# Norm factors of q and k spread by TensorE, and bias rows of the sample group as long runs, in a one-core decoder layer

## The chip, the core and the metric

The kernel runs on one core of a Trainium2 chip. A core has five engines, each with its own in-order queue of instructions: TensorE (PE in the profile, with its weight loads as PEld), VectorE (DVE), ScalarE (ACT), GpSimd (POOL) and SyncE (SP), which here only issues transfers. Transfers are carried out by 16 DMA engines; those issued by SP form one queue, those issued by POOL another. The metric is the device time of one execution, in microseconds. Lower is better.

## The reference

One layer of a decoder that serves a prompt of 1024 tokens and 8 sample sequences of 8 tokens each, so 1088 tokens in all, with a model width of 1024:

```
a  = silu(c) @ w_ada + b_ada                  # 6 x 1024 shifts, scales, gates, per sequence
h  = rms_norm(x, g1) * (1 + scale1) + shift1
q, k, v, u = split(h @ w_in)                  # 512 columns each; q, k, v: 8 heads of 64
q  = rms_norm(q, q_g) * 64**-0.5              # by head
k  = rms_norm(k, k_g)
attn = three dilated window branches (window, step) = (128,1), (512,4), (2048,16),
       each softmax(q k + bias[bucket(distance)]), merged by their denominators;
       sample tokens read a cache of 2048 keys as well
pool = (trailing mean over 2/4/8/16 tokens - token) @ w_pool * pool_scale
x  = x + gate1 * (concat(attn, pool) @ w_out)
x  = x + gate2 * (relu(rms_norm(x) ... @ w_up)**2 @ w_down)
```

Outputs are the new x, the new k and v, the pooling input and the shifted caches. Everything is fp32. The norm by head is what the change touches: each head's 64 rows of q (or k) are multiplied, token by token, by one factor 1/sqrt(mean of squares + eps), and by a gain.

## The kernel before

Activations lie with features on the 128 partitions and the 1088 tokens along the free dimension. The tokens are cut into three chunks of 512, 288 and 288 columns (`CHUNKS`), since a PSUM bank holds 512 fp32 values per partition. There are eight such banks, all of one tag in the first phase (`ps`).

**Precision.** A product with a weight tile is made of three fp32r matmuls: the weight is split on the chip into a high part (ScalarE, L145) and the rest (VectorE, L146), the activations likewise, and high x high, low x high and high x low are summed (`gemm`, L236 to L245). Small products are plain fp32; each of those shows as two records in the profile.

**The order of work.** The source is traced in program order, and a scheduler (`schedule_with_timeline_sim=True`, L928) then chooses each engine's order by a model of the time, keeping the program order as priority and allotting the buffers. So neighbours in the source can be interleaved, and the engines' real queues are read from the trace.

**The start.** Eight tiles of x are loaded (L169), then `rel_bias`, and for a table of the bias by distance, in blocks of 1024 columns (`G0`, L176), a one-hot block `oh` and a block `lm` with the log of the number of branches (L180, L181). Distances number `GLEN` = 2312, so there are three blocks. Block n has its rows at partitions 32n. Small matmuls `pg` (L222) pick the bias, five in all, ScalarE copies them (L226), POOL adds them to `lm` (L300). The norm of x follows on TensorE (`n1`, L203). Once h is made, POOL writes the table to DRAM 16 times over (`gscr`, L305).

**The input projection** is the stage that the change is in. Its 16 column tiles of 128 are taken in the order k (tiles 4 to 7), q (0 to 3), u (12 to 15), v (8 to 11). `in_tile` (L309) loads a weight tile on SP's queue (`win4r` and so on, 512 KB), splits it, and multiplies into three PSUM banks `z`. It then takes two steps of the later part of the ada product (`ada_steps`, L117): each step loads a block of 512 KB on SP's queue (`wa`, L95) and multiplies it on TensorE (`pa`, L100). Eight steps share one PSUM bank `pa`; when the next eight begin, the old sum is copied and transposed (`pat`, L109). The weight blocks and the ada blocks share four buffers (`NRAW`).

`qk_group` (L321) runs four tiles, for k and then for q. For each tile VectorE copies z out of PSUM (L328) and ScalarE squares it (L329). After the fourth, twelve small matmuls against `sel` add the squares of each head (L337): the sums of tile r's two heads stand in rows 32r and 32r + 1. VectorE scales them (L338), and `rsqrt` (L136) with a Newton step (L131) gives the factors `rst`. POOL writes these to DRAM (`kscr` or `qscr`, four transfers of two rows, L342). SP reads each pair of rows back, repeated 64 times, as a full tile `rb` of 128 rows (L345). VectorE multiplies each tile with its gain and `rb` (L346). After the k group POOL writes k out (L352).

After the q group SP loads the bias rows of the sample tokens from `gscr`: `bs` for the cached keys and `bnew` for the new ones, by head pair (L360 to L372). A key of the cache is far if it is only in the branch of step 16: 96 groups of 8 keys, laid out group by group in the key tiles. A sample token's far bias is then 96 runs of 8 values (32 bytes each) in the table (L364 to L366).

u follows with the pooling sums on POOL (`pool_group`, L376), and its last pieces go out (`out_up` L380, `out_us` L412). Then v. After that come attention (phase 2), the output projection (phase 3) and the channel sub-layer (phase 4).

Of the kernel before, what the change touches and what calls it, by code (L numbers as in the profile page):

```python
# [38 lines left out]
GLEN = 2312  # L39
GREP = 16  # L40
# [8 lines left out]
def body(ctx: ExitStack, tc: tile.TileContext, i, o):  # L49
# [28 lines left out]
    cT, bT, g1T, g2T, qkg, ident, ones, sel, pscT, rcnt = (part(n) for n in CPK)  # L78
# [38 lines left out]
    def ada_steps():  # L117
        """the later 4096 columns, one block of rows a step"""
        done = None
        for r in (1, 2):  # L120
            for hf in range(2):
                pa = ps(f"pa{r}_{hf}")
                for k in range(KD):
                    ada_mm(pa, k, ada_load(r, hf, k, wpool, "raw", NRAW))
                    if k == 0 and done:
                        ada_end(*done)
                    yield
                done = (r, hf, pa)
        ada_end(*done)
# [6 lines left out]
    def rsqrt(r, v, t):  # L136
        """r = 1/sqrt(v)"""
# [34 lines left out]
    gscr = tc.dram_tile([H, GREP, GLEN], F32, name="gscr")  # L172
    rbias = const.tile([32, H], F32, tag="rbias", name="rbias")
    nc.sync.dma_start(rbias, i["rel_bias"])
    lm = nat_pool.tile([P, 1024], F32, tag="nat", name="lm")
    G0 = [(32 * n, c0, min(1024, GLEN - c0)) for n, c0 in enumerate(range(0, GLEN, 1024))]  # L176
# [19 lines left out]
    def rstd_of(acc, rstd, chunks, name):  # L196
        """rstd = 1/sqrt(mean + eps) on every partition, from the sums acc over feature blocks"""
# [105 lines left out]
    with tc.issue_after(ins.ins):  # L303
        for r0, c0, n in G0:
            G.dma_start(gscr[:, :, c0:c0 + n], lm[r0:r0 + H, :n].unsqueeze(1).to_broadcast([H, GREP, n]))  # L305

# [14 lines left out]
    def qk_group(base, gvec, name):  # L321
        """four tiles of two heads each: the projection, then the norm by head"""
        raws, sqs = [], []
        for r in range(4):
            outs = in_tile(base + r)
            t, sq = nat(f"{name}{r}"), nat(f"{name}sq{r}")
# [3 lines left out]
            raws.append(t)  # L330
            sqs.append(sq)
        rst = nat(f"{name}rst")
        vv, tv = nat(f"{name}vv"), nat(f"{name}tv")
        for ci, (c0, n) in enumerate(CHUNKS):
            pp = ps(f"{name}ss{ci}")
            for r in range(4):
                mm(pp[32 * r:32 * r + 32, :n], sel, sqs[r][:, c0:c0 + n], start=True, stop=True)  # L337
            V.tensor_scalar(vv[:, c0:c0 + n], pp[:, :n], 1.0 / E, EPS, ALU.mult, ALU.add)  # L338
        rsqrt(rst, vv, tv)
        scr = tc.dram_tile([H, T], F32, name=f"{name}scr")  # L340
        for r in range(4):
            G.dma_start(scr[2 * r:2 * r + 2, :], rst[32 * r:32 * r + 2, :])  # L342
        for r in range(4):
            rb = nat(f"{name}rb{r}")
            nc.sync.dma_start(rb, bass.AP(tensor=scr.tensor, offset=2 * r * T, ap=[[T, 2], [0, E], [1, T]]))  # L345
            V.scalar_tensor_tensor(raws[r], raws[r], gvec, rb, ALU.mult, ALU.mult)  # L346
        return raws

    kT = qk_group(4, gk, "k")

    for r in range(4):
        G.dma_start(o["kT"][r], kT[r])  # L352
    qT = qk_group(0, gq, "q")

# [5 lines left out]
    for hp in range(HP):  # L360
        r0 = 32 * hp
        g0 = 2 * hp * GREP * GLEN + TS - 1
        for a in range(2):
            nc.sync.dma_start(bs[r0 + a * TS:r0 + (a + 1) * TS, 0:NFAR].rearrange("p (n r) -> p n r", r=TS),  # L364
                              bass.AP(tensor=gscr.tensor, offset=g0 + a * GREP * GLEN,
                                      ap=[[GLEN - 1, TS], [16, 96], [1, TS]]))  # L366
        nc.sync.dma_start(bs[r0:r0 + 16, NFAR:NKEY],
                          bass.AP(tensor=gscr.tensor, offset=g0 + WB - NEAR,
                                  ap=[[GREP * GLEN, 2], [GLEN - 1, TS], [1, NEAR]]))
        nc.sync.dma_start(bnew[r0:r0 + 16, 7 * TS:8 * TS],  # L370
                          bass.AP(tensor=gscr.tensor, offset=g0 + WB,
                                  ap=[[GREP * GLEN, 2], [GLEN - 1, TS], [1, TS]]))  # L372
# [36 lines left out]
    for r in range(4):  # L409
        uT.append(in_copy(12 + r, f"u{r}"))  # L410
        pool_group(r)
    nc.sync.dma_start(o["us"], us[:, :, :, TS:])  # L412

    # v by token: a tile for each head pair, eight blocks of 128 tokens; the sample tokens of all heads
# [37 lines left out]
    def head_prep(h, pieces):  # L452
        """q and k of a head in two parts each: rows of the head, and the other rows"""
# [19 lines left out]
    # ================= phase 2: attention =================  # L473
# [13 lines left out]
    # sample queries by head pair: columns (head of the pair, token) over the rows of that head  # L487
# [15 lines left out]
    def softmax_tail(L, n, negm, name):  # L503
        """L holds minus the logits: L <- exp(logit - max); returns 1/sum"""
# [17 lines left out]
    def sample_S(b):  # L522
        """logits by 512 keys a step, then the softmax"""
# [21 lines left out]
    def sample_V(b):  # L545
        """the product with V by four tiles of 128 keys a step"""
# [403 lines left out]
```

## Time and profile before

| | |
|---|---|
| median of 3 runs | 1434.34 us (1432.61 to 1436.79) |
| span of the profiled execution | 1432.4 us |
| PE busy | 1316.1 us, 92% |
| PEld busy | 1130.7 us, 79% |
| DVE busy | 607.4 us, 42% |
| ACT busy | 402.6 us, 28% |
| POOL busy | 135.3 us, 9% |

The profile is of one further execution, whose span is the only time it has. Its views: the page (busy shares, and the span in 40 slices), who waited for whom, the chain of waits that ended last, the groups of instructions by line, the timeline of each engine, and the busy time, granted TensorE clock and DMA share in chosen stretches. In a timeline row the first number is the start, the second the length, both in us; `L337` is a line of the kernel; `z<-h1h,win2h` is output from inputs; `x3` counts records that were merged; `[11.07 <-ACT ...]` is the idle time before the row and what ended it. Rows of SPq are transfers being issued. A granted clock of 1.00 is full speed. DMA share is the mean busy share of the 16 engines.

### The profile page before, as it was taken

How to read it: one execution, taken by the hardware profiler on the slowest of the kernel's cores; microseconds unless marked ns; L12 is line 12 of the kernel's file. 1: busy time of each engine (PE TensorE's matmuls, PEld its weight loads, DVE VectorE, ACT ScalarE, POOL GpSimd, SP SyncE). 2: the span in 40 equal slices, each digit the busy share in tenths (PEclk: the TensorE clock that was granted, in tenths of full speed). 3: DMA queues.
4: the chain of work that ended last, by engine and by line, in shares of the span. 5: the costliest groups of instructions: out<-in, count | busy, mean ns of one | idle time of the engine just before them, and what ended most of it. 6: DMA issues, size and time to landing. Idle time of an engine off the chain costs nothing.

```text
span 1432.4 us, 21960 instructions
## 1 busy us (share of the span) xinstructions
PE 1316.1 (92%) x9230; PEld 1130.7 (79%) x9230; DVE 607.4 (42%) x1250; ACT 402.6 (28%) x705; POOL 135.3 (9%) x193
## 2 busy tenths in 40 slices
PE   3798469279899999999999999999999999999998
PEld 1586358168677776899999999999999999999998
DVE  5632121321576777465643343342433433424333
ACT  5322021011567676343420211202112112021120
POOL 2100000351232221000000000000000000000000
PEclk9899689599999999999999999999999999999999
DMA  9673432394986772556493181351631813511102
GB/s 296 236 94 90 143 129 80 106 137 139 329 270 237 254 259 64 208 168 216 157 331 113 45 278 44 131 193 44 222 102 45 278 45 132 191 47 43 45 17 109
DMA packets 65826, 217.27 MB, mean 152 GB/s; under 512 B 20824, under 2 KB 23040, under 8 KB 64704
## 3 DMA queue, kind: packets, MB, share of 16 engines
q1 hardware_dynamic: 62416, 143.31, 31.6%
q0 software_dynamic: 3312, 72.56, 15.7%
q8 instruction: 73, 1.20, 0.3%
q14 instruction: 25, 0.20, 0.0%
HBM read 203.31 MB, written 77.29 MB: 196 GB/s over the span
## 4 chain that ended last, share of the span: by engine, by line
PE 75%; ACT 2%; DMA 1%; DVE 1%; SPq 1%; issue 0%; POOL 0%; ACTq 0%; DVEq 0%; POOLq 0%
PE dn L243 9%; PE dn L241 9%; PE dn L245 9%; PE up L241 9%; PE up L243 9%; PE up L245 9%; PE po L617 2%; PE pt L612 2%; PE spo L566 1%; PE sl L533 1%; PE z L243 1%; PE ob L245 1%; PE ob L241 1%; PE ob L243 1%; PE z L245 1%; PE z L241 1%
## 5 line engine op out<-in xcount | busy, mean ns | idle before, releaser
L699 DVE SCALAR_TENSOR_TENSOR X<-dn,aT,X 128x512 f32<-128x512 f32 (+2 forms) x192 | 98.4, 567 | 204.6 <-PE dn L245 204.6
L731 POOL COPY mark<-fh 128x1 f32<-128x1 f32 x7 | 8.5, 1220 | 562.1 <-ACT fh L798 562.1
L617 PE MATMUL po<-PT,vtok 128*64 128x128 f32 x576 | 52.2, 287 | 4.7 <-ACT PT L615 3.9
L799 DVE TENSOR_TENSOR fl<-r,fh 128x1088 fp32r<-128x1088 f32 x32 | 41.3, 1292 | 35.5 <-ACT fh L798 35.5
L506 ACT ACTIVATE L<-L,m 128x128 f32<-128x128 f32 (+3 forms) x64 | 49.8, 778 | 22.5 <-DVE m L512 22.0
L617 PEld LDWEIGHTS po<-PT,vtok 128*64 128x64 f32 x576 | 33.7, 136 | 24.1 <-ACT PT L615 13.6
L100 PE MATMUL pa<-wa,cs 128*32 128x256 f32 x384 | 29.5, 407 | 22.6 <-DMA wa<-in_w_ada 22.5
L798 ACT CAST fh<-r 128x1088 fp32r<-128x1088 f32 x32 | 35.4, 1106 | 44.1 <-DVE r L795 44.1
L615 ACT COPY PT<-pt 128x512 f32<-128x512 f32 (+1 forms) x80 | 40.2, 541 | 15.6 <-PE pt L612 15.4
L243 PE MATMUL dn<-fh,wd_3l 128*128 128x288 f32 (+1 forms) x192 | 43.4, 328 | 0.0
L241 PE MATMUL dn<-fh,wd_3h 128*128 128x288 f32 (+1 forms) x192 | 43.4, 328 | 0.0
L245 PE MATMUL dn<-fl,wd_3h 128*128 128x288 f32 (+1 forms) x192 | 43.4, 328 | 0.0
L241 PE MATMUL dn<-fh,wd_1h 128*128 128x288 f32 (+1 forms) x192 | 42.5, 328 | 0.0
L243 PE MATMUL dn<-fh,wd_1l 128*128 128x288 f32 (+1 forms) x192 | 42.5, 328 | 0.0
L245 PE MATMUL dn<-fl,wd_1h 128*128 128x288 f32 (+1 forms) x192 | 42.3, 328 | 0.0
L243 PE MATMUL dn<-fh,wd_0l 128*128 128x288 f32 (+1 forms) x192 | 42.3, 328 | 0.0
L612 PE MATMUL pt<-cpk,L 128*128 128x128 f32 x288 | 41.6, 281 | 0.7 <-ACT L L506 0.4
L241 PE MATMUL dn<-fh,wd_0h 128*128 128x288 f32 (+1 forms) x192 | 42.2, 328 | 0.0
L243 PE MATMUL dn<-fh,wd_2l 128*128 128x288 f32 (+1 forms) x192 | 42.2, 328 | 0.0
L241 PE MATMUL dn<-fh,wd_2h 128*128 128x288 f32 (+1 forms) x192 | 42.2, 328 | 0.0
L245 PE MATMUL dn<-fl,wd_2h 128*128 128x288 f32 (+1 forms) x192 | 42.2, 328 | 0.0
L245 PE MATMUL dn<-fl,wd_0h 128*128 128x288 f32 (+1 forms) x192 | 42.1, 328 | 0.0
(947 smaller groups left out, 3482.9 us busy)
## 6 DMA issues: line engine op xcount, KB each, us to landing
out_kw<-in_cache_k POOLq DMA_DIRECT2D x8, 4080.0 KB, 15.6
out_vw<-in_cache_v POOLq DMA_DIRECT2D x8, 4080.0 KB, 28.6
wa<-in_w_ada SPq DMA_DIRECT2D x48, 512.0 KB
kc<-in_kc SPq DMA_DIRECT2D x40, 512.0 KB
vc<-in_vc SPq DMA_DIRECT2D x40, 512.0 KB
x<-in_xT SPq DMA_DIRECT2D x8, 544.0 KB
X<-in_xT SPq DMA_DIRECT2D x8, 544.0 KB
fs<-gscr SPq DMA_DIRECT2D x8, 512.0 KB
```

The source lines that it names most:

```text
L100: ins = mm(pa[32 * g:32 * g + 32, :256], cs[:, k, :], t[:, g // 2, (g % 2) * 256:(g % 2 + 1) * 256], start=(k == 0), stop=(k == KD - 1))
L241: mm(pt[:, :n], wh[:, kw], xh(k, c0, n), start=st, stop=False)
L243: mm(pt[:, :n], wl[:, kw], xh(k, c0, n), start=False, stop=False)
L245: mm(pt[:, :n], wh[:, kw], xl(k, c0, n), start=False, stop=sp)
L506: last["act"] = S.activation(L[:, :n], L[:, :n], AF.Exp, bias=negm, scale=-1.0, accum_out=sm)
L533: mm(pt[32 * hp:32 * hp + 32, c0:c0 + 256], qz[:, hp, b, :], kch[:, hp, :], start=True, stop=True)
L612: nc.tensor.transpose(pt[:, n * P:(n + 1) * P], Ls[ii][:, j * P:(j + 1) * P], ident)
L615: S.copy(PT[:, :w], pt[:, :w])
L617: mm(po[E * ii:E * ii + E, :P], v_blk(j, h * E, E), PT[:, n * P:(n + 1) * P], start=(j == 0), stop=(j == 2 * g + ii))
L699: V.scalar_tensor_tensor(X[:, m, c0:c0 + npr], pt[:, :npr], aT[:, base + m, 0:1], X[:, m, c0:c0 + npr], ALU.mult, ALU.add)
L798: S.copy(fh, r)
L799: V.tensor_sub(fl, r, f(fh))
```

## The change

1. `qk_group` becomes a class `QK` with three steps: `tile(r)`, `stats()` (up to the factors `rst`, as before) and `scale()`. `scale()` sends nothing through DRAM. For each chunk of tokens it takes four PSUM banks and lets TensorE multiply, for each tile r, a constant 32 x 128 matrix `selb` (one in row 0 for the first 64 columns, one in row 1 for the last 64) with rows 32r to 32r + 31 of `rst`. So each bank holds one tile's factors, spread to its 128 rows, and VectorE multiplies the tile with its gain and that bank, in place.
2. The scale stands one tile later in the source: k's after the first q tile, q's after the first u tile. k's four output transfers (POOL) follow k's scale.
3. The far keys of the cache are laid out by shift, all 96 groups of one of the eight positions after another (`rows`, on the host, for keys and values). A second table `fscr` of 15 x 96 distances is made beside the first, by the same matmuls, copies and additions, and written once to DRAM. A sample token's far bias is then one run of 768 values, so one transfer of 16 rows per head pair replaces two of 768 short runs.
4. The table grows from 2312 to 3752 columns: four blocks in place of three, eight matmuls `pg` in place of five.
5. The loads of `bs` and `bnew` move from SP's queue to POOL's: 12 transfers.
6. `selb` joins the packed constants. Comments are dropped.

```diff
+FLEN = 15 * 96
...
+    fscr = tc.dram_tile([H, FLEN], F32, name="fscr")
...
-    G0 = [(32 * n, c0, min(1024, GLEN - c0)) for n, c0 in enumerate(range(0, GLEN, 1024))]
+    G0 = [(32 * n, c0, min(1024, GLEN + FLEN - c0)) for n, c0 in enumerate(range(0, GLEN + FLEN, 1024))]
...
         for r0, c0, n in G0:
-            G.dma_start(gscr[:, :, c0:c0 + n], lm[r0:r0 + H, :n].unsqueeze(1).to_broadcast([H, GREP, n]))
+            ng = max(0, min(n, GLEN - c0))
+            if ng:
+                G.dma_start(gscr[:, :, c0:c0 + ng], lm[r0:r0 + H, :ng].unsqueeze(1).to_broadcast([H, GREP, ng]))
+            if ng < n:
+                f0 = c0 + ng - GLEN
+                G.dma_start(fscr[:, f0:f0 + n - ng], lm[r0:r0 + H, ng:n])
...
-        scr = tc.dram_tile([H, T], F32, name=f"{name}scr")
-        for r in range(4):
-            G.dma_start(scr[2 * r:2 * r + 2, :], rst[32 * r:32 * r + 2, :])
-        for r in range(4):
-            rb = nat(f"{name}rb{r}")
-            nc.sync.dma_start(rb, bass.AP(tensor=scr.tensor, offset=2 * r * T, ap=[[T, 2], [0, E], [1, T]]))
-            V.scalar_tensor_tensor(raws[r], raws[r], gvec, rb, ALU.mult, ALU.mult)
-        return raws
...
+        def scale(self):
+
+            for c0, n in CHUNKS:
+                c = slice(c0, c0 + n)
+                rbs = [ps(f"{self.name}rb{r}_{c0}") for r in range(4)]
+                for r in range(4):
+                    mm(rbs[r][:, :n], selb[32 * r:32 * r + 32, :], self.rst[32 * r:32 * r + 32, c], start=True, stop=True)
+                for r in range(4):
+                    V.scalar_tensor_tensor(self.raws[r][:, c], self.raws[r][:, c], self.gvec, rbs[r][:, :n], ALU.mult, ALU.mult)
+
+    kg, qg = QK(4, gk, "k"), QK(0, gq, "q")
+    kT, qT = kg.raws, qg.raws
+    for r in range(4):
+        kg.tile(r)
+    kg.stats()
+    qg.tile(0)
+    kg.scale()
     for r in range(4):
         G.dma_start(o["kT"][r], kT[r])
-    qT = qk_group(0, gq, "q")
...
+    for r in range(1, 4):
+        qg.tile(r)
+    qg.stats()
...
-        for a in range(2):
-            nc.sync.dma_start(bs[r0 + a * TS:r0 + (a + 1) * TS, 0:NFAR].rearrange("p (n r) -> p n r", r=TS),
-                              bass.AP(tensor=gscr.tensor, offset=g0 + a * GREP * GLEN,
-                                      ap=[[GLEN - 1, TS], [16, 96], [1, TS]]))
-        nc.sync.dma_start(bs[r0:r0 + 16, NFAR:NKEY],
+        G.dma_start(bs[r0:r0 + 16, 0:NFAR],
+                    bass.AP(tensor=fscr.tensor, offset=2 * hp * FLEN + 7 * 96,
+                            ap=[[FLEN, 2], [-96, TS], [1, NFAR]]))
+        G.dma_start(bs[r0:r0 + 16, NFAR:NKEY],
...
-        nc.sync.dma_start(bnew[r0:r0 + 16, 7 * TS:8 * TS],
+        G.dma_start(bnew[r0:r0 + 16, 7 * TS:8 * TS],
...
         uT.append(in_copy(12 + r, f"u{r}"))
+        if r == 0:
+            qg.scale()
         pool_group(r)
...
-    rows = np.concatenate([(16 * np.arange(96)[:, None] + np.arange(TS)[None]).ravel(), np.arange(WB - NEAR, WB)])
+    rows = np.concatenate([(16 * np.arange(96)[None] + np.arange(TS)[:, None]).ravel(), np.arange(WB - NEAR, WB)])
...
+    selb = np.zeros((P, P), np.float32)
+    selb[0::32, :E] = 1
+    selb[1::32, E:] = 1
```

More of the change, by code (lines that the diff above doesn't have):

```diff
@@ L76, in part @@
         return v
-    cT, bT, g1T, g2T, qkg, ident, ones, sel, pscT, rcnt = (part(n) for n in CPK)
+    cT, bT, g1T, g2T, qkg, ident, ones, sel, selb, pscT, rcnt = (part(n) for n in CPK)
     gq = const.tile([P, 1], F32, tag="gq", name="gq")
@@ L319, in in_tile, with __init__, tile @@
         return outs
-    def qk_group(base, gvec, name):
-        raws, sqs = [], []
-        for r in range(4):
-            outs = in_tile(base + r)
-            t, sq = nat(f"{name}{r}"), nat(f"{name}sq{r}")
+    class QK:
+        def __init__(self, base, gvec, name):
+            self.base, self.gvec, self.name = base, gvec, name
+            self.raws, self.sqs = [], []
+        def tile(self, r):
+            outs = in_tile(self.base + r)
+            t, sq = nat(f"{self.name}{r}"), nat(f"{self.name}sq{r}")
             for pt, (c0, n) in zip(outs, CHUNKS):
@@ L329, in qk_group @@
                 S.activation(sq[:, c0:c0 + n], pt[:, :n], AF.Square)
[L330 to L335, printed above, removed]
-            for r in range(4):
-                mm(pp[32 * r:32 * r + 32, :n], sel, sqs[r][:, c0:c0 + n], start=True, stop=True)
-            V.tensor_scalar(vv[:, c0:c0 + n], pp[:, :n], 1.0 / E, EPS, ALU.mult, ALU.add)
@@ L339, in qk_group @@
-        rsqrt(rst, vv, tv)
-        scr = tc.dram_tile([H, T], F32, name=f"{name}scr")
-        for r in range(4):
-            G.dma_start(scr[2 * r:2 * r + 2, :], rst[32 * r:32 * r + 2, :])
-        for r in range(4):
-            rb = nat(f"{name}rb{r}")
-            nc.sync.dma_start(rb, bass.AP(tensor=scr.tensor, offset=2 * r * T, ap=[[T, 2], [0, E], [1, T]]))
-            V.scalar_tensor_tensor(raws[r], raws[r], gvec, rb, ALU.mult, ALU.mult)
-        return raws
-    kT = qk_group(4, gk, "k")
+            self.raws.append(t)
@@ new lines, in tile, with stats @@
+            self.sqs.append(sq)
+        def stats(self):
+            name = self.name
+            rst = self.rst = nat(f"{name}rst")
+            vv, tv = nat(f"{name}vv"), nat(f"{name}tv")
+            for ci, (c0, n) in enumerate(CHUNKS):
+                pp = ps(f"{name}ss{ci}")
+                for r in range(4):
+                    mm(pp[32 * r:32 * r + 32, :n], sel, self.sqs[r][:, c0:c0 + n], start=True, stop=True)
+                V.tensor_scalar(vv[:, c0:c0 + n], pp[:, :n], 1.0 / E, EPS, ALU.mult, ALU.add)
+            rsqrt(rst, vv, tv)
@@ L351, in body @@
+    kT, qT = kg.raws, qg.raws
+    for r in range(4):
+        kg.tile(r)
+    kg.stats()
+    qg.tile(0)
+    kg.scale()
     for r in range(4):
         G.dma_start(o["kT"][r], kT[r])
-    qT = qk_group(0, gq, "q")
+    for r in range(1, 4):
+        qg.tile(r)
+    qg.stats()
     bs = side.tile([P, NKEY], F32, tag="bs", name="bs")
@@ L834 @@
 for _n, _s in (("cT", (KD, 9)), ("bT", (48,)), ("g1T", (KD,)), ("g2T", (KD,)), ("qkg", (2,)), ("ident", (P,)),
-               ("ones", (P,)), ("sel", (32,)), ("pscT", (4,)), ("rcnt", (4, CTX))):
+               ("ones", (P,)), ("sel", (32,)), ("selb", (P,)), ("pscT", (4,)), ("rcnt", (4, CTX))):
     CPK[_n] = (NCPK, _s)
@@ L851, in _distance_tables @@
 def _distance_tables():
-    dist = GOFF - np.arange(GLEN)
+    far = WB + 7 - np.arange(15)[:, None] - 16 * np.arange(96)[None]
+    dist = np.concatenate([GOFF - np.arange(GLEN), far.ravel()])
     d = np.maximum(dist, 1).astype(np.float32)
@@ L859, in _distance_tables @@
     logm = np.where(n > 0, np.log(np.maximum(n, 1)), BIG).astype(np.float32)
-    return onehot, np.ascontiguousarray(np.broadcast_to(logm, (H, GLEN)))
+    return onehot, np.ascontiguousarray(np.broadcast_to(logm, (H, GLEN + FLEN)))
 def _tiles(w, m):
@@ L894 @@
         "sel": sel,
+        "selb": selb,
         "pscT": col(pool_scale, 4),
```

## The prediction

> **What bounds the kernel now.** I read the page first: the engine totals, then the forty slices, each 35.8 us long.
>
> ```profile
> span 1432.4 us, 21960 instructions
> ...
> PE 1316.1 (92%) x9230; PEld 1130.7 (79%) x9230; DVE 607.4 (42%) x1250; ACT 402.6 (28%) x705; POOL 135.3 (9%) x193
> ...
> PE   3798469279899999999999999999999999999998
> ...
> PEclk9899689599999999999999999999999999999999
> ```
>
> TensorE is the bound, and from the tenth slice on it has hardly a hole. The holes are in the slices from 143 to 322 us (digits 4, 6, 9, 2, 7), where the input projection runs, and there the granted clock falls as well. So I asked who TensorE waited for up to 380 us (columns: total us, times, longest).
>
> ```profile
> PE z L241 <- ACT qsq L329: 25.3, 1, 25.3
> PE pa L100 <- DMA wa<-in_w_ada: 22.5, 5, 12.9
> PE z L241 <- ACT win15h L145: 12.7, 1, 12.7
> PE z L241 <- ACT win3h L145: 11.1, 1, 11.1
> PE z L243 <- DVE win15l L146: 2.3, 1, 2.3
> ```
>
> Then the same stretch by stages: length, busy time of each engine, granted clock, DMA share, GB/s.
>
> ```profile
> 72.00:138.00 66.00, 66.00 (x424) 53.85 (x422) 20.22 (x32) 15.58 (x23) 4.19 (x8) 1.00 0.59 95
> 164.00:170.00 6.00, 6.00 (x21) 5.40 (x22) 0.00 (x0) 0.33 (x2) 0.00 (x0) 0.53 0.32 128
> 190.50:197.00 6.50, 6.50 (x20) 5.49 (x21) 2.52 (x4) 1.20 (x3) 0.00 (x0) 0.51 0.86 303
> 197.00:250.50 53.50, 53.50 (x352) 43.17 (x350) 11.95 (x15) 11.09 (x15) 3.58 (x8) 1.00 0.30 92
> 277.30:286.00 8.70, 6.42 (x21) 5.45 (x22) 5.32 (x9) 0.88 (x3) 7.53 (x6) 0.52 0.45 161
> 316.00:320.00 4.00, 3.78 (x23) 1.96 (x23) 0.30 (x2) 0.66 (x1) 0.00 (x0) 0.53 1.02 411
> 252.00:260.00 8.00, 0.00 (x0) 0.00 (x0) 1.30 (x2) 0.00 (x0) 2.68 (x4) 0.68 0.13 52
> ```
>
> Two things are to be seen. Left alone, this stage keeps TensorE full: 66.00 us busy of 66.00, and 53.50 of 53.50 at a DMA share of 0.30. And after each long wait it works for 6 to 9 us at half clock. The last row is the middle of a hole: for 8 us nothing runs on TensorE, and the DMA share is 0.13, two engines' worth of sixteen.
>
> Whose are the holes? For the first I read the timelines of VectorE and ScalarE.
>
> ```profile
> 149.01 1.35 DVE L346 SCALAR_TENSOR_TENSOR k<-k,cpk,krb 128x1088 f32<-128x1088 f32 x1 [15.30 <-DMA krb<-kscr]
> 161.14 1.35 DVE L346 SCALAR_TENSOR_TENSOR k<-k,cpk,krb 128x1088 f32<-128x1088 f32 x1 [10.78 <-DMA krb<-kscr]
> 162.41 1.41 DVE L328 COPY q<-z 128x512 f32<-128x512 f32 x3
> ```
>
> VectorE works in order. The copies that empty the accumulators of q1 (L328) stand behind two scalings of k that wait for the broadcast read `krb`; the square (L329) waits for the copy, the next z tile for the bank, and TensorE stands 25.3 us. One broadcast (128 x 1088 x 4 B) lands about every 12 us (149.01, 161.14); at the 52 GB/s of the two busy engines it would take 10.7. The others are seen on SP's queue.
>
> ```profile
> 161.35 10.68 SPq L151 DMA_DIRECT2D win3r<-in_w_in  x1
> ...
> 247.40 2.77 SPq L345 DMA_DIRECT2D qrb<-qscr  x1
> 250.27 9.65 SPq L380 DMA_DIRECT2D out_up<-u  x1
> 259.97 0.77 SPq L151 DMA_DIRECT2D win15r<-in_w_in  x1
> ...
> 296.22 0.65 SPq L412 DMA_DIRECT2D out_us<-us  x1
> ```
>
> `win3r` takes 10.68 us to issue behind the last `krb`, `win15r` goes out 9.65 us late behind the last `qrb`. I therefore give the waits for win3 (11.1), win15 (12.7 and 2.3) and the 12.9 of the ada load to the broadcasts too. Of the 22.5 us, another wait has a different cause:
>
> ```profile
> 315.87 1.08 PE L100 MATMUL pa<-wa,cs 128*32 128x256 f32 x8 [6.99 <-DMA wa<-in_w_ada]
> ```
>
> These 7.0 us follow `out_us` at 296.22, which the change leaves where it is.
>
> **The change, part by part.** *The round trip of the factors goes* (8 small writes on POOL's queue, 8 broadcasts on SP's). Idle time that goes: 25.3 + 11.1 + 12.9 + 12.7 + 2.3 = 64.3 us. Half-clock work that goes with it: 6.00 x (1 - 0.53) + 6.50 x (1 - 0.51) + 6.42 x (1 - 0.52) = 2.8 + 3.2 + 3.1 = 9.1 us. Together 73.4 us. What stays is the hole after `out_us`, 7.0 us, and its half clock, 4.00 x 0.47 = 1.9: 8.9 us that I don't take. What is late next is TensorE itself, by the two full stages above.
>
> *TensorE spreads the factors*: per group 12 fp32 matmuls of 32 rows, four for each chunk, each over 1088 columns in all. The nearest rows are full-array fp32 matmuls over 512 and 576 columns (chain of waits), and the sums by head, where four matmuls use four column slices (PE's timeline).
>
> ```profile
> 621.39 0.86 PE n2a L203 x2
> 672.62 0.97 PE n2b L203 x4
> ...
> 206.59 2.00 PE L337 MATMUL qss<-qsq,cpk 128*32 128x512 f32 x18
> ...
> 112.04 0.67 PE L337 MATMUL kss<-ksq,cpk 128*32 128x288 f32 x2
> ```
>
> One factor block costs 0.86 + 0.97 = 1.83 us, so eight blocks one after another cost 14.6 us; if four run side by side, 2 x 1.83 = 3.7. The 18 records of L337 are nine matmuls; in turn they'd take about 5.9 us (four at 0.86, five at about half of 0.97), and they took 2.00, so slices do run together by columns. For slices by rows no row exists. I take 6.0, nearer to the L337 row, keep 3.7 and 14.6 for the range, and exclude a gain, since nothing on TensorE is dropped.
>
> The Trainium skill (TensorEngine Tiling (Array Packing), Key Properties and Gotcha 1) says that row slices run in parallel if they write different PSUM banks, but that a change of tiling mode drains the array. By its parallel rule alone the term would be 3.7 and the sum 2.3 us lower; that a drain is dear no run here shows.
>
> *VectorE scales out of PSUM*: 12 pieces per group in place of four whole tiles.
>
> ```profile
> L699 DVE SCALAR_TENSOR_TENSOR X<-dn,aT,X 128x512 f32<-128x512 f32 x64 | 48.1, 751 | 202.7 <-PE dn L245 202.7
> L699 DVE SCALAR_TENSOR_TENSOR X<-dn,aT,X 128x288 f32<-128x288 f32 x64 | 32.5, 508 | 0.8 <-PE dn L245 0.8
> ```
>
> The same operation on the same shapes: 4 x 0.751 + 8 x 0.508 = 7.1 us per group, against 4 x 1.35 = 5.4. In the full stage of 53.50 us VectorE is busy 11.95, so 1.7 more lies beside the matmuls. What is new is how it is tied to the banks: of eight, a scale holds four, the z tile three, the ada sum one, and where an ada sum is changed for the next (tiles q0 and u0, just ahead of both scales) two more are wanted. A z tile, or the next chunk's scale, can then wait for VectorE. Queued behind that wait on TensorE are the following z tile and the ada matmuls, and everything later. Bounds: nothing, if z work is placed between the chunks; 7.1 us a group if TensorE stands through the whole drain. I take 2 a group, 4.0 in all, nearer to nothing, because the scheduler already places such pieces singly between z's, as it did with the L337 pair of 112.04.
>
> The factors must be ready when TensorE comes to the scale:
>
> ```profile
> 123.33 0.64 PE L100 MATMUL pa<-wa,cs 128*32 128x256 f32 x8
> ...
> 131.08 1.29 DVE L134 SCALAR_TENSOR_TENSOR krst<-ktv,krst 128x1088 f32<-128x1088 f32 x1
> ...
> 219.90 1.29 DVE L134 SCALAR_TENSOR_TENSOR qrst<-qtv,qrst 128x1088 f32<-128x1088 f32 x1
> ...
> 223.13 0.64 PE L100 MATMUL pa<-wa,cs 128*32 128x256 f32 x8
> ```
>
> q's end at 221.2, u0's products at 223.1: covered. k's end at 132.4, q0's products at 123.3: not covered as it stands, by 9.1 us. But k's chain started late, and why is the next part.
>
> *The bias rows go to POOL's queue, as long runs.*
>
> ```profile
> SPq L364 <- DMA gscr<-lm: 28.1, 1, 28.1
> ...
> 116.75 0.37 SPq L151 DMA_DIRECT2D win1r<-in_w_in  x1
> ...
> 122.27 1.23 DVE L146 TENSOR_TENSOR win1l<-win1r,win1h 128x1024 fp32r<-128x1024 f32 x1 [15.39 <-ACT win1h L145]
> ```
>
> SP stands 28.1 us for the distance table, then issues the rows until 116.7, and only then `win1r`. VectorE stood 15.39 us at the split of win1, with k's mean (L338) in its queue behind that, although the last sums by head ran soon after the pair of 112.04. From the split to k's factors went 8.9 us (123.5 to 132.4). With the rows off SP, `win1r` goes out up to 28 us sooner, the chain can begin at about 114, and k's factors come at about 123, just in time. TensorE was full through that stage (66.00 of 66.00), so nothing else is gained. The early loads now share the engines with the table's write. What covers that: the next of them are needed at about 123 us (the ada row above), and SP's wait shows the table landing long before. On POOL the twelve row loads, two small writes of the far table and four `out_kT` stand in a queue that is busy 4.19 us of 66.00; the rows are first read in the attention. All this I cost at nothing; if the cover went, the k scale's 9.1 us would come back.
>
> *The longer table at the start*: one more block of one-hot and log rows, and eight small matmuls instead of five ahead of norm1's sums.
>
> ```profile
> 12.85 0.31 SPq L180 DMA_DIRECT2D oh<-in_onehot  x1
> ...
> 17.87 4.47 PE L222 MATMUL pg<-oh,rbias 32*8 32x512 f32 x10 [17.87 <-DMA oh<-in_onehot]
> ```
>
> If the three extra matmuls ran in turn: 4.47 x 3/5 = 2.7 us; if beside the others in their own column slice, nothing. The pairs of loads on SP are 2.7 us apart, the same bound. I take 1.5, with 0 and 2.7 as ends.
>
> Sum: -73.4 + 6.0 + 4.0 + 1.5 = -61.9, from the span of 1432.4 to 1370.5. The median of the runs shown, 1434.3, is 1.9 above that span; I add this and forecast **1372.4 us**.
>
> **The rivals.** (A) *A new wait at the scales*: k's factors stay 9.1 us late and TensorE waits for the banks through both drains, 14.2, with some 3 us at half clock behind the longer one: 26.3 in place of 4.0, so 1394.7. For it speaks that ten banks are wanted where eight exist, and that the order comes from a model of time; against it, that 2.00 us for 18 records shows pieces well placed. (B) *The loads are late of themselves*: only the hole made by VectorE goes, 25.3 + 2.8, and the four waits for loads come back elsewhere: 1434.3 - 28.1 + 11.5 = 1417.7. Against it: a DMA share of 0.13 while TensorE waits, and full stages at 0.30. (C) *Slower*: the 24 matmuls are scattered among z's, and each change between a row slice and the full array empties it. It decides from (73.4 - 5.5) / 24 = 2.8 us for each; at 3.5 it gives 1372.4 - 6.0 + 84.0 = 1450.4. The scattered L337 pair of 112.04 took 0.67 where half of 0.97 is 0.49: 0.2 of overhead, though by columns. (D) *No change*: the queue orders come out such that a wait of the old size, some 30 us, meets each group: about 1434.
>
> **How the numbers follow.** Forecast 0.70, A 0.15, B 0.09, C 0.03, D 0.03. Low end: 3.7 for the spread, no stall, no longer start, and the hole after `out_us` gone too: 1434.3 - 73.4 + 3.7 - 8.9 = 1355.7. High end: A, with 1394.7, and a little of the dearer spread, 1396. B, C and D are left out, 0.15. A measurement of this kernel can tell about 0.3% from no change, 4.3 us. Faster than that: forecast, A, B, 0.94; within it D, 0.03; slower C, 0.03.
>
> **What would show it.** Right: no wait of z on `qsq`, on win3 or win15, and no 12.9 us wait on `wa`; granted clock 1.00 from 72 us to the hole after `out_us`; VectorE never idle for a DMA between the k and q groups; SP's loads of weights issued in under 1 us; attention beginning some 62 us sooner; everything from there as long as before. A shows as TensorE waiting on VectorE's scaling or on `krst`, B as `wa` or `win` waits at a DMA share above 0.5, C as gaps around the 24 matmuls. The forecast is wrong if the full stages don't stay full once nothing interrupts them.

## The result, and the profile after

| | before | after |
|---|---|---|
| median of four runs | 1435.57 us (1432.61 to 1436.91) | 1384.44 us (1379.98 to 1386.11) |
| span of the profiled execution | 1432.4 us | 1383.9 us |
| first score matmul of the attention (`S`) | 361.42 us | 311.60 us |

The ratio is 0.9643 (95% interval 0.9623 to 0.9664): 51 us faster, where 62 were forecast. The direction and the range held; the forecast of 1372.4 was 12 us too low. The page of after, slices of 34.6 us:

```profile
span 1383.9 us, 22069 instructions
...
PE 1323.1 (96%) x9284; PEld 1133.3 (82%) x9284; DVE 609.9 (44%) x1266; ACT 404.1 (29%) x708; POOL 142.2 (10%) x200
...
PE   3799999798999999999999999999999999999998
...
PEclk9799999899999999999999999999999999999999
```

The slices in which before had 4, 6, 9, 2 and 7 now have 9, 9, 9, 7 and 9; the 7 lies at about 242 to 277 us. TensorE's waits up to 380 us (us in total, times, longest):

```profile
PE pa L101 <- DMA wa<-in_w_ada: 14.9, 8, 9.2
PE z L243 <- ACT h1h L265: 10.0, 1, 10.0
...
PE qrb L361 <- DVE q L363: 0.4, 1, 0.4
```

The waits on `qsq`, win3 and win15 and the 12.9 us on `wa` are gone, all of them. What is left is the hole after `out_us` (9.2), and one that has grown: before the first z, TensorE now waits 10.0 us for `h1h`, where it waited 4.66. By stages (length, busy time of each engine, granted clock, DMA share, GB/s):

```profile
129.00:134.60 5.60, 4.28 (x46) 1.69 (x42) 3.66 (x6) 1.44 (x3) 0.00 (x0) 1.00 0.93 274
134.60:144.90 10.30, 9.79 (x37) 6.70 (x34) 5.00 (x10) 1.04 (x1) 2.19 (x4) 0.50 0.87 284
145.00:195.00 50.00, 50.00 (x310) 42.10 (x308) 11.82 (x17) 10.68 (x16) 0.00 (x0) 1.00 0.23 82
...
257.50:271.20 13.70, 5.92 (x29) 3.86 (x30) 1.48 (x3) 1.04 (x1) 0.00 (x0) 0.50 0.95 251
311.60:1383.90 1072.30, 1057.60 (x7585) 927.28 (x7583) 496.49 (x1099) 323.84 (x587) 69.29 (x98) 1.00 0.46 154
```

Between the two scales TensorE is full (50.00 of 50.00), as forecast. Around the k scale it runs at half clock for 10.3 us, which was not forecast. From the first `S` to the end there are 1072.3 us, and before had 1071.0, so the whole gain, 49.8 us up to the first `S`, is made ahead of the attention.

The two places that cost more than forecast are seen in TensorE's timeline and in those of VectorE and POOL. On TensorE (start, length, both us): the first z, the first sums by head, the k scale, and the ada load after `out_us`:

```profile
42.55 1.03 PE L243 MATMUL z<-h1h,win4h 128*128 128x512 f32 x2 [9.97 <-ACT h1h L265]
...
110.36 0.59 PE L351 MATMUL kss<-ksq,cpk 128*32 128x512 f32 x1
...
129.13 1.13 PE L361 MATMUL krb<-krst,cpk 32*128 32x512 f32 x6
...
131.20 1.61 PE L361 MATMUL krb<-krst,cpk 32*128 32x512 f32 x12
134.13 0.65 PE L101 MATMUL pa<-wa,cs 128*32 128x256 f32 x8 [1.32 <-DMA wa<-in_w_ada]
134.71 1.64 PE L361 MATMUL krb<-krst,cpk 32*128 32x288 f32 x4
136.87 1.08 PE L101 MATMUL pa<-wa,cs 128*32 128x256 f32 x8 [0.51 <-DMA wa<-in_w_ada]
137.88 1.32 PE L361 MATMUL krb<-krst,cpk 32*128 32x288 f32 x2
139.13 0.80 PE L243 MATMUL z<-h1h,win1h 128*128 128x512 f32 x1
...
264.59 1.08 PE L101 MATMUL pa<-wa,cs 128*32 128x256 f32 x8 [9.15 <-DMA wa<-in_w_ada]
```

The Newton step of the first norm on VectorE, after's and then before's:

```profile
29.93 3.52 DVE L133 SCALAR_TENSOR_TENSOR n1t<-rstd 128x512 f32<-128x512 f32 x2 [3.10 <-ACT rstd L212]
33.37 2.77 DVE L134 TENSOR_TENSOR n1t<-n1t,n1v 128x512 f32<-128x512 f32 x2
36.07 3.49 DVE L135 SCALAR_TENSOR_TENSOR rstd<-n1t,rstd 128x512 f32<-128x512 f32 x2
```
```profile
30.01 1.36 DVE L132 SCALAR_TENSOR_TENSOR n1t<-rstd 128x512 f32<-128x512 f32 x2 [2.69 <-ACT rstd L210]
31.29 1.35 DVE L133 TENSOR_TENSOR n1t<-n1t,n1v 128x512 f32<-128x512 f32 x2
32.56 1.35 DVE L134 SCALAR_TENSOR_TENSOR rstd<-n1t,rstd 128x512 f32<-128x512 f32 x2
```

And POOL's additions into the bias table, again after and before:

```profile
25.29 9.64 POOL L302 TENSOR_TENSOR lm<-lm,fb 8x1024 f32<-8x1024 f32 x4 [7.48 <-DMA wa<-in_w_ada]
```
```profile
24.11 5.60 POOL L300 TENSOR_TENSOR lm<-lm,fb 8x264 f32<-8x264 f32 x3 [6.39 <-ACT fb L226]
```

In before the additions end at 29.71, just ahead of the Newton step at 30.01. In after they start 1.2 us later, are longer by the fourth block and run to 34.93, over the first two of the step's three rows. Over the third runs POOL's split of `win4` (L147). The three rows take 9.6 us in place of 3.9. Each row is two instructions, over 512 and 576 columns. Taken singly, and put in order of time with POOL's, two of the six are:

```profile
30.16 2.68 POOL L302 TENSOR_TENSOR lm<-lm,fb 8x1024 f32<-8x1024 f32 x1
30.55 2.89 DVE L133 SCALAR_TENSOR_TENSOR n1t<-rstd 128x576 f32<-128x576 f32 x1
...
36.35 2.59 POOL L147 TENSOR_TENSOR win4l<-win4r,win4h 128x1024 fp32r<-128x1024 f32 x1 [0.81 <-ACT win4h L146]
36.67 2.89 DVE L135 SCALAR_TENSOR_TENSOR rstd<-n1t,rstd 128x576 f32<-128x576 f32 x1
```

In each row one instruction takes its usual 0.7 us and the other 2.1 to 2.9. The long ones end 0.5 to 0.6 us after the POOL instruction beside which they began (33.44 behind 32.84, 35.47 behind 34.93, 39.56 behind 38.94). So this looks like waiting until POOL's instruction is over, and not like slower work throughout.

### The profile page after: what moved, and what is told of

Read it like the earlier page. It is cut to its first block, busy times and chain, and to the rows that moved or that the text cites. A ratio compares the mean times of both kernels' runs of the same rounds, so it can differ in the third digit from the quotient of the medians.

```text
span 1383.9 us, 22069 instructions
## 1 busy us (share of the span) xinstructions
PE 1323.1 (96%) x9284; PEld 1133.3 (82%) x9284; DVE 609.9 (44%) x1266; ACT 404.1 (29%) x708; POOL 142.2 (10%) x200
## 4 chain that ended last, share of the span: by engine, by line
PE 89%; DMA 4%; ACT 2%; DVE 2%; issue 2%; SPq 1%; POOL 0%; ACTq 0%; DVEq 0%
PE dn L243 9%; PE dn L245 9%; PE dn L247 9%; PE up L247 9%; PE up L243 9%; PE up L245 9%; PE z L243 5%; PE z L247 4%; PE z L245 4%; PE po L641 2%; DMA wa<-in_w_ada 2%; PE pt L636 2%; PE sl L557 1%; PE pa L101 1%; PE ob L245 1%
## 5 line engine op out<-in xcount | busy, mean ns | idle before, releaser
L530 ACT ACTIVATE L<-L,m 128x128 f32<-128x128 f32 (+3 forms) x64 | 49.8, 778 | 22.2 <-DVE m L536 22.0
L641 PEld LDWEIGHTS po<-PT,vtok 128*64 128x64 f32 x576 | 33.7, 136 | 23.4 <-ACT PT L639 12.9
L101 PE MATMUL pa<-wa,cs 128*32 128x256 f32 x384 | 31.5, 414 | 15.0 <-DMA wa<-in_w_ada 14.9
```

The costliest lines, as they stand in the source:

```text
L101: ins = mm(pa[32 * g:32 * g + 32, :256], cs[:, k, :], t[:, g // 2, (g % 2) * 256:(g % 2 + 1) * 256], start=(k == 0), stop=(k == KD - 1))
L530: last["act"] = S.activation(L[:, :n], L[:, :n], AF.Exp, bias=negm, scale=-1.0, accum_out=sm)
L641: mm(po[E * ii:E * ii + E, :P], v_blk(j, h * E, E), PT[:, n * P:(n + 1) * P], start=(j == 0), stop=(j == 2 * g + ii))
```

## The experiments

My theory after this: the holes came from the broadcast reads, which the two outer rows of their access pattern hold to two DMA engines; whatever cures that gets the gain, and the scales on TensorE are one cure, at a price. Rivals: the loads were late of themselves (B of the prediction); the gain comes from the scale being one tile later; the bias rows did the work; the 24 small matmuls are dear in themselves (C). All ratios are against before on the same chip, with 95% intervals; where two changed kernels are compared, their ratios are subtracted and taken of 1433 us. Such a difference is uncertain by 4 to 6 us (the half widths of the two intervals, squared, added, and the root taken), so a difference of a few microseconds shows nothing by itself. The runs are called e1 to e7 and e9 to e13.

**Which half.** e1: the bias part alone, put into before (longer table, far table, `rows`, loads on POOL):

```diff
-            nc.sync.dma_start(bs[r0 + a * TS:r0 + (a + 1) * TS, 0:NFAR].rearrange(...), <gscr, 768 runs>)
+        G.dma_start(bs[r0:r0 + 16, 0:NFAR], <fscr, 16 rows>)
```

> The kernel before with only the second half of the change: far keys by shift, far table, and the bias rows on POOL's queue; the factors still go through DRAM. Theory (the holes come from the broadcasts on two DMA engines): the holes stay; k's factors come about 9 us sooner and the start costs about 4, so 1426 to 1440. Rival (the bias rows on SP's queue make the loads late): most of the gain is here, below 1405.

1434.16 us, ratio 1.0004 (0.999 to 1.0019): no change, and the holes of before are there. TensorE's waits up to 380 us:

```profile
PE z L243 <- ACT qsq L336: 19.0, 1, 19.0
PE z L243 <- ACT win15h L146: 12.8, 1, 12.8
PE z L243 <- ACT win3h L146: 12.5, 1, 12.5
```

e2: the other half, after with the old table and the old bias loads on SP:

```diff
-        G.dma_start(bs[r0:r0 + 16, 0:NFAR], <fscr, 16 rows>)
+            nc.sync.dma_start(bs[r0 + a * TS:r0 + (a + 1) * TS, 0:NFAR].rearrange(...), <gscr, 768 runs>)
```

> The changed kernel with the old bias rows (short runs, SP's queue, short table). Theory: the holes are gone, the start is 4 us shorter than in the changed kernel, but k's factors come some 5 to 9 us late for their scale: 1380 to 1395. Rival (bias rows make the holes): above 1410.

1381.32 us, 0.963 (0.9595 to 0.9665): the whole change's gain. Here the k factors do come late, as the prediction's rival A had it, and the clock is halved behind that (waits; then the stretch 127.7 to 148.2):

```profile
PE krb L354 <- DVE krst L134: 5.6, 1, 5.6
```
```profile
127.70:148.20 20.50, 16.58 (x73) 8.79 (x74) 13.98 (x22) 3.18 (x5) 2.19 (x4) 0.50 0.67 219
```

In after this wait is absent, but the longer table delays the start by about as much (first z at 38.11 here, 42.55 in after). So the bias part buys the k factors in time and pays for it at the start. Together that is 2 us against after (1433 x 0.0013), which the runs can't tell from nothing.

**Is it the read's access pattern?** e3: before with one edit: each factor row is written to DRAM eight times, so that the same 544 KB tile is read by 16 outer rows instead of 2.

```diff
-        scr = tc.dram_tile([H, T], F32, name=f"{name}scr")
+        scr = tc.dram_tile([H, 8, T], F32, name=f"{name}scr")
-            G.dma_start(scr[2 * r:2 * r + 2, :], rst[32 * r:32 * r + 2, :])
+            G.dma_start(scr[2 * r:2 * r + 2, :, :], rst[32 * r:32 * r + 2, :].unsqueeze(1).to_broadcast([2, 8, T]))
-            ... offset=2 * r * T, ap=[[T, 2], [0, E], [1, T]]
+            ... offset=16 * r * T, ap=[[T, 16], [0, 8], [1, T]]
```

> The kernel before with one edit: the factors are written to DRAM eight times over, so that the broadcast read has 16 outer rows in place of 2; order and place of the scaling unchanged. Theory (two engines carry a read with two outer rows): each read takes about 3 us in place of 12, the waits for win3, win15 and wa go, the hole at q1 shrinks from 25 to some 10 us: 1365 to 1385. Rival (loads are late of themselves, or any trip through DRAM stalls VectorE): above 1405.

1373.4 us, 0.9588 (0.9555 to 0.962): these lines alone gain 60 us, more than the whole change (8 us more, 1433 x 0.0055). VectorE's timeline shows why:

```profile
139.99 1.35 DVE L346 SCALAR_TENSOR_TENSOR k<-k,cpk,krb 128x1088 f32<-128x1088 f32 x1 [9.60 <-DMA krb<-kscr]
143.93 1.35 DVE L346 SCALAR_TENSOR_TENSOR k<-k,cpk,krb 128x1088 f32<-128x1088 f32 x1 [2.58 <-DMA krb<-kscr]
...
150.36 1.35 DVE L346 SCALAR_TENSOR_TENSOR k<-k,cpk,krb 128x1088 f32<-128x1088 f32 x1 [1.16 <-DMA krb<-kscr]
```

k's scalings stand 2.6 to 3.9 us apart, in before 12 to 14 (149.01, 161.14, 174.90, 188.07). While these reads run, from 137 to 148 us, the DMA share is 1.03 to 1.06 and 275 to 301 GB/s move (the share is rough and can exceed 1). The wait on `qsq` is 7.6 us, and win3 and win15 are not waited for. B falls: the loads were late because of the broadcasts. The Trainium skill (DMA: Bandwidth & Descriptors, Rules for kernel authors, the row on using all 16 engines) states this rule: an outermost dimension of c under 16 confines a transfer to at most c engines. The trace agrees: a DMA share of 0.13, two of sixteen, with two outer rows.

e11: the scale one tile later, as in after, but through DRAM with the old two-row read:

```diff
...
-                    mm(rbs[r][:, :n], selb[32 * r:32 * r + 32, :], self.rst[32 * r:32 * r + 32, c], ...)
...
+                nc.sync.dma_start(rb, bass.AP(tensor=scr.tensor, offset=2 * r * T, ap=[[T, 2], [0, E], [1, T]]))
```

> The changed kernel with the scale one tile later, but through DRAM by the old read with two outer rows. Theory (the two engines are what matters; the place of the scale alone cures little): the loads of weights are late as before, 1410 to 1436. Rival (taking the scale one tile later is what frees VectorE, whatever the read): 1370 to 1395.

1431.98 us, 0.9991 (0.9977 to 1.0004): nothing, as long as the read is slow (with the fast read it is another matter: e13 against e12, below). The holes only change their names (waits):

```profile
PE pa L101 <- DMA wa<-in_w_ada: 39.4, 10, 13.1
...
PE z L243 <- ACT win3h L146: 13.6, 1, 13.6
PE z L243 <- ACT win15h L146: 12.7, 1, 12.7
```

**What the scales on TensorE cost.** e4: after with its scale sent through DRAM by the 16-row read, at the same place in the source:

```diff
...
-                    mm(rbs[r][:, :n], selb[32 * r:32 * r + 32, :], self.rst[32 * r:32 * r + 32, c], ...)
...
+                nc.sync.dma_start(rb, bass.AP(tensor=scr.tensor, offset=16 * r * T, ap=[[T, 16], [0, 8], [1, T]]))
+                V.scalar_tensor_tensor(self.raws[r], self.raws[r], self.gvec, rb, ALU.mult, ALU.mult)
```

> The changed kernel, but with its scale one tile later done through DRAM with the 16-row read, so nothing on TensorE for it. Theory (in the changed kernel the two scales cost TensorE some 14 us and a clock drop of 3): 1362 to 1374. Rival (the trip through DRAM holds VectorE and with it the banks, whatever the engines): above 1390.

1371.02 us, 0.9565 (0.9539 to 0.9592): 11 us less than after (1433 x 0.0078), although its first z is later still (45.07 us). So the scales on TensorE cost some 11 us more, with 5 either way, than a well-spread read, which TensorE hardly waits for: in its list of waits there is none on `qsq`, and 1.0 and 0.5 us on win3.

e7: after with each spreading matmul done twice, the same values into the same bank:

```diff
-                for r in range(4):
+                for r in (0, 1, 2, 3, 0, 1, 2, 3):
                     mm(rbs[r][:, :n], selb[32 * r:32 * r + 32, :], ...)
```

> The changed kernel with every one of the 24 spreading matmuls issued twice into the same bank. It prices the matmuls alone, since banks and VectorE's work stay. If four run side by side: 4 us more, 1388. If they are scattered and each pays for itself as in the trace (about 5 us a group): 8 to 11 more, 1392 to 1396. If a change to row slices is dear (2 us or more each): above 1420.

1400.27 us, 0.9765 (0.9748 to 0.9783), 17 us more than after (1433 x 0.0122). This is between the cases named, and the total alone would have misled me; the rows tell them apart (TensorE's timeline):

```profile
207.82 2.96 PE L361 MATMUL qrb<-qrst,cpk 32*128 32x512 f32 x28
214.12 4.77 PE L361 MATMUL qrb<-qrst,cpk 32*128 32x288 f32 x20 [2.79 <-DVE q L363]
```

28 records are 14 matmuls, eight over 512 columns and six over 288; one after another at the prediction's 0.86 and 0.97 / 2 they'd take 9.8 us, and they took 2.96. So row slices that write different banks do run side by side, 3.3 at a time by this row, and no change of slice is dear; rival C, which needs 2.8 us for each matmul, falls. What the doubling adds are waits for banks that VectorE still drains (6.4 and 2.8 us in all) and half clock behind them (139.2 to 152.8, 214.3 to 224.5).

**The start.** e5: after with POOL's additions moved behind the first norm, directly ahead of the table's write:

```diff
-    for r0, c0, n in G0:
-        G.tensor_add(lm[r0:r0 + H, :n], lm[r0:r0 + H, :n], fb[r0:r0 + H, :n])
     with tc.issue_after(ins.ins):
+        for r0, c0, n in G0:
+            G.tensor_add(lm[r0:r0 + H, :n], lm[r0:r0 + H, :n], fb[r0:r0 + H, :n])
```

> The changed kernel with one edit: POOL's four additions to the distance table are held behind the mark that starts the table's write, so that they don't run beside VectorE's Newton steps for norm1. Theory (the start lost 5.5 us because POOL's longer additions slowed VectorE's steps from 3.9 to 9.6 us): the first z starts at about 38 us in place of 42.6, and 4 to 5 us go: 1378 to 1381. Rival (the start is late because of the longer loads and matmuls themselves): no change, 1383 to 1386.

1385.34 us, 0.9648 (0.9621 to 0.9674): a miss, with no gain that the runs show, though with 5 us either way they don't exclude the 4 us forecast. The start is mended (the three rows of the Newton step take 1.36, 1.35 and 1.35 again, the first z is at 39.79 in place of 42.55), and half of that is lost again by the first `S` (310.2 for 311.6). SP's and ScalarE's timelines, the stretch 100 to 106, and TensorE's waits:

```profile
88.41 0.34 SPq L152 DMA_DIRECT2D win1r<-in_w_in  x1
```
```profile
113.71 1.05 ACT L146 CAST win1h<-win1r 128x1024 fp32r<-128x1024 f32 x1 [24.52 <-DMA win1r<-in_w_in]
```
```profile
100.00:106.00 6.00, 6.00 (x38) 5.45 (x37) 0.00 (x0) 0.00 (x0) 0.00 (x0) 1.00 0.96 51
```
```profile
PE kss L351 <- ACT ksq L340: 5.3, 1, 5.3
```

The table's write goes out at 86.4 and keeps the engines at a share of 0.96 while only 51 GB/s move. `win1r` goes out 2 us behind it, and its split is reached only at 113.71; k's last squares stand behind that split in ScalarE's queue, and TensorE waits 5.3 us for them. In after the write goes out at 79.28 and `win1r` at 110.57, when the table has landed. This is the cover that the prediction gave the early loads; here it failed.

**The hole after `out_us`.** e6: after with the state packed on POOL before it goes out, so that each partition writes rows of 1920 bytes instead of runs of 60:

```diff
-    nc.sync.dma_start(o["us"], us[:, :, :, TS:])
+    usc = wpool.tile([P, 4, NB, CTX], F32, tag="tmp", name="usc", bufs=2)
+    for g in range(4):
+        G.tensor_copy(usc[:, g], us[:, g, :, TS:])
+    nc.sync.dma_start(o["us"], usc)
```

> The changed kernel with one edit: the pooling state of the sample group is copied by POOL into one dense tile and written out from there, in rows of 1920 bytes in place of 4096 runs of 60. Theory (those short runs keep all DMA engines for some 16 us and the ada loads behind them come late): the 9.2 us wait for the ada load and the half clock behind it go, 10 to 13 us: 1371 to 1375. Rival (the loads after the last u tile are late of themselves): 1382 to 1386.

1372.35 us, 0.9578 (0.9558 to 0.9599): 9 us gained (1433 x 0.0065). The waits on `wa` fall from 14.9 to the following; below it, the stretch of after in which the short runs go out:

```profile
PE pa L101 <- DMA wa<-in_w_ada: 4.3, 4, 1.4
```
```profile
252.00:257.00 5.00, 3.44 (x31) 2.42 (x29) 1.88 (x5) 1.16 (x3) 2.21 (x5) 1.00 1.30 27
```

In after the engines are busy throughout while 27 GB/s move. In e6, with the packed write among the transfers, 209 to 409 GB/s move (256 to 264 us). But the edit also moves the write: it goes out at 256.28, behind the loads of win10 and win11, where after has it at 242.81, ahead of two ada blocks. What the later place is worth alone was not tried.

**Together.** e9: after with the 16-row read in place of the matmuls, the late additions and the packed state:

```diff
+                nc.sync.dma_start(rb, bass.AP(tensor=scr.tensor, offset=16 * r * T, ap=[[T, 16], [0, 8], [1, T]]))
...
+            G.tensor_add(lm[r0:r0 + H, :n], lm[r0:r0 + H, :n], fb[r0:r0 + H, :n])
...
+    nc.sync.dma_start(o["us"], usc)
```

> The changed kernel with the scale through DRAM by the 16-row read, the additions behind the mark and the dense pooling state, all three together. If the three causes are separate: 1371 less 4 to 5 less 10 to 13, 1353 to 1358. If one hides another: 1360 to 1367.

1351.49 us, 0.9433 (0.9416 to 0.945): the best version of all, 30 us ahead of after (1433 x 0.021) and a little below the forecast for separate causes. The first full stretch of the projection:

```profile
128.00:150.00 22.00, 22.00 (x143) 19.34 (x142) 7.96 (x8) 3.27 (x5) 2.20 (x4) 1.00 0.97 293
```

TensorE is full at full clock here, at a DMA share of 0.97, and stays so up to the attention (50.00 of 50.00 us from 150 on, then 78.84 of 79.00). The late additions do no harm here: `win1r` goes out at 85.59, ahead of the table's write at 87.03, and is split at 94.93.

e10: that version with the additions where after has them:

```diff
+    for r0, c0, n in G0:
+        G.tensor_add(lm[r0:r0 + H, :n], lm[r0:r0 + H, :n], fb[r0:r0 + H, :n])
     with tc.issue_after(ins.ins):
-        for r0, c0, n in G0:
-            G.tensor_add(lm[r0:r0 + H, :n], lm[r0:r0 + H, :n], fb[r0:r0 + H, :n])
```

> The version with all three edits, but with POOL's additions where the changed kernel has them: beside VectorE's Newton steps. Theory (POOL's longer additions cost the start 5 us and more): 1356 to 1361, against 1351.5 with the additions held back. Rival (holding them back did nothing for the time, as the run of that edit alone showed no gain): 1350 to 1353.

1359.34 us, 0.9489 (0.9469 to 0.951): with the additions beside the Newton step the kernel is 8 us slower (1433 x 0.0056). Half of it is explained: the wait on `h1h` is 8.9 us, with the additions late it is 4.6, and the first `S` comes 3.8 us later (283.0 for 279.2). In the profiles 6.1 us more arise behind the first `S` (1076.0 to the end for 1069.9), and why is not shown.

e12: with the 16-row read and the packed state, but the old bias loads on SP and the short table, whose additions stand where before has them:

```diff
-        G.dma_start(bs[r0:r0 + 16, 0:NFAR], <fscr, 16 rows>)
+            nc.sync.dma_start(bs[r0 + a * TS:r0 + (a + 1) * TS, 0:NFAR].rearrange(...), <gscr, 768 runs>)
```

> The kernel with the scale one tile later through DRAM by the 16-row read and the dense pooling state, but with the old bias rows: short runs, SP's queue, short table. Theory (the bias half is worth nothing on TensorE and its longer table costs the start): 1349 to 1356, as fast as the best version with the new bias rows, 1351.5. Rival (freeing SP's queue is worth its few us once the other holes are gone): 1358 to 1365.

1365.48 us, 0.953 (0.9509 to 0.9552): 14 us behind the best version (1433 x 0.0097), 6 behind the one without late additions (1433 x 0.0041), which was the rival's forecast and not mine. With the larger holes gone, SP's queue counts. TensorE's waits, and SP's queue:

```profile
PE z L241 <- ACT win3h L145: 4.8, 1, 4.8
```
```profile
99.96 0.97 SPq L381 DMA_DIRECT2D bs<-gscr  x2
...
114.50 0.45 SPq L151 DMA_DIRECT2D win1r<-in_w_in  x1
...
136.84 0.60 SPq L356 DMA_DIRECT2D krb<-kscr  x1
...
141.30 0.54 SPq L151 DMA_DIRECT2D win3r<-in_w_in  x1
```

The rows hold back `win1r` to 114.50, k's factors follow late, and `win3r` goes out behind the last `krb`. Against e10 (rows on POOL, additions in the same place) the first z is 4.3 us sooner (37.70 for 42.05), but the first `krb` goes out 4.9 us later (136.84 for 131.95), and TensorE waits longer for loads: 7.6 us for 2.8 on `wa`, 4.8 for 0.8 on `win3h`. The first `S` is 5.0 us later (288.0 for 283.0).

e13: last, before with only the two small edits, the 16-row read and the packed state:

```diff
+            ... offset=16 * r * T, ap=[[T, 16], [0, 8], [1, T]]
...
+    nc.sync.dma_start(o["us"], usc)
```

> The kernel before with two small edits only: the 16-row read of the factors and the dense pooling state; scale where it was, bias rows where they were. From 1373.4 by the gain that the dense state had in the changed kernel, 12: 1359 to 1364. What it lacks against the version above is the scale one tile later, so it keeps the 7.6 us hole at q1 and its half clock.

1371.08 us, 0.9573 (0.9555 to 0.9592): a miss, since the packed state brought 2 us here (1433 x 0.0015, against e3) and 9 in after; with 5 and 4 us either way the two are barely apart. In the profiles the first `S` comes 4.7 us sooner than without the packed state (293.0 for 297.7), though the hole was 7.5; k's factors came 2.8 us later and the wait on `qsq` grew from 7.6 to 9.2. Of the 4.7, all but 1.8 was lost again behind the first `S`. Why, I can't say: the attention's waits on `kc` are 2.2 us longer in that profile (3.0 for 0.8), and nothing was tried on it.

e13 differs from e12 in the place of the scale alone (and in the constant `selb`, which e12 loads and does not use), and e12 is 6 us faster (1433 x 0.0043, 4 either way), with its first `S` 5.0 us sooner (288.0 for 293.0). So once the read is fast, taking the scale one tile later is worth some 6 us: in e12 no wait on `qsq` is left, where e13 has 9.2.

## Why the prediction was right, and where its sizes were off

The forecast's mechanism held: the broadcasts made the holes, and with them the holes went. What the change itself costs was put too low in every term. From the two profiles:

| term | forecast | measured |
|---|---|---|
| holes and half clock of the round trip | -73.4 | -73.4: every wait named is gone |
| longer table at the start | 1.5 | 4.3: the first `kss` at 110.36, before 106.08 |
| both scales on TensorE | 6.0 + 4.0 | 14.2, and 2.9 at half clock behind k's |
| hole after `out_us` | 0 (stays) | 3.7: waits 9.15 + 0.69 for 6.99 + 0.22, half clock 3.0 for 1.9 |
| from the first `S` on | 0 | 1.3 |
| sum | -61.9 | -47.0; the spans differ by 48.5, so 1.5 is in no row |

- **The round trip.** Right. From the first `kss` to the first `S` TensorE stood 71.5 us in before and 12.1 in after, and what is left is the hole after `out_us` and 2.2 us at the scales. e3 shows the cause that the prediction read from the DMA share of 0.13: two engines. That the step stands one tile later brought nothing beside the slow read (e11), and some 6 us beside the fast one (e12 and e13).
- **The scales.** This is the term that was mis-sized most. k's takes from 129.13 to 139.13, 10.0 us, with four ada steps that cost 2.1 anywhere: 7.9. q's takes from 196.71 to 205.13, less 2.1: 6.3. In k's, TensorE shows 1.13 + 1.61 + 1.64 + 1.32 = 5.7 us of spreading matmuls, in q's 4.9, so 10.6 in both. "I take 6.0, nearer to the L337 row" is the step that failed. It is not that slices are slow: e7 has 14 in 2.96 us. They go in runs of one to six, with ada matmuls between. The rest are short waits (at k 1.8 us for ada blocks, at q 0.4 for a bank) and ada steps that take longer among them. Behind k's scale the z matmuls run at half clock to 144.9, 5.8 x 0.5 = 2.9 us. This is not rival A: A put 14.2 us of waiting for banks on top of the 6.0 for the matmuls, and the wait for banks is 0.4. Only its 3 us at half clock came.
- **The signs.** The sign of a granted clock of 1.00 up to the hole failed, around k's scale and from 73.2 to 76.6 us. The attention begins 49.8 us sooner in place of 62. The other signs of being right came.
- **k's factors.** Forecast just in time, and so they were, but with luck: they are ready at 126.8 where 123 was forecast, and q0's products slipped alike, to 127.6 from 123.3. `win1r` goes out 6.2 us sooner (110.57 for 116.75), not 28: SP then stands 13.5 us for TensorE's ada matmuls just ahead of it. Without the bias part the factors are 5.6 us late (e2).
- **The start.** The step that failed is "if the three extra matmuls ran in turn", the only price that the term was given. The eight `pg` matmuls take 4.65 us against 4.47, so they cost nothing; the cost is POOL's fourth addition, which I hadn't priced, and with which the additions reach into VectorE's Newton step; the step's end then falls beside POOL's next split. e9 against e10 shows it by its removal: 8 us, of which some 4 are seen at the start. In after alone the removal shows no gain (e5); there the table's write then meets `win1r`.
- **Bias rows at nothing.** Right for this change (e1, e2), but only because larger holes hid it: once they are gone the part is worth 6 us (e12 against e10, 4 either way), 14 with the late additions. The cover for the early loads holds where `win1r` goes out ahead of the table's write (85.59 in e9) or after the table has landed (110.57 in after), and fails in between (88.41 in e5).
- **The hole after `out_us`** stayed, as said; that it grew from 7.0 to 9.15 I don't explain. That the short runs make it is borne out by e6, though the write's later place there has a share that was not measured.

## What to carry to other kernels

Where a transfer is slow while the DMA share is low, look at the outermost dimension of its access pattern before moving the work to another engine: here a few lines in before brought 60 us where the rewritten step brought 51. A gain of nothing for one part (the bias rows, the scale one tile later) holds only while larger holes cover it, so it is worth trying parts again once the large ones are gone. And an operation that is moved or lengthened on an idle engine has a price on its neighbours: read what runs beside it in the same microseconds.

## What the runs showed of the hardware

- A broadcast of 544 KB with two outer rows lands every 10.6 to 13.8 us (before, by the scalings of k and q), with 16 outer rows every 2.4 to 4.4 (e3).
- Three fp32 instructions of VectorE with two inputs in SBUF, over 512 or 576 columns of 128 partitions, took 2.1 to 2.9 us in place of 0.7: each began beside an instruction of POOL with two inputs and ended 0.5 to 0.6 us after it (after, 30 to 40 us). Two of the POOL instructions were additions over only 8 partitions. POOL loses little: 1024 columns take it 2.68 us beside VectorE's step and 2.37 ahead of it. The Trainium skill (GPSIMD Engine Reference, Key points) says that POOL and VectorE share their SBUF interfaces and contend where VectorE has two SBUF inputs; the trace agrees, since these do.
- The clock was halved from 134.6 us although TensorE's longest gap in the 5.6 us before was 1.32 us and the stretch as a whole was 76% busy (4.28 of 5.60); it then stayed so for 10.3 us at 95% busy. The Trainium skill (TensorE: Matmul & The Clock Gate, A second HAM failure mode) describes short idle gaps between groups of matmuls that cycle through PSUM banks as enough to throttle; this fits, but no run separates the small gaps from the small row slices.
- A 16-fold table write from 8 partitions a block holds the DMA engines at a share of 0.96 while 51 GB/s move (100 to 106 us in e5). `win1r`, issued 2 us behind it, lands after 25.2 us; in after, where it goes out when the table has landed, after 5.0.
- 4096 runs of 60 bytes hold the engines at a share of 1.30 while 27 GB/s move (252 to 257 us in after).
